# Seven block products in place of eight for three quarters of a decoder trunk's second feed-forward product

## The chip, the core and the metric

The kernel runs on one core of one Trainium2 chip. The metric is the device time of one execution in microseconds (us), as the median over several runs. Engines are written as in the profile: PE is TensorE (matmuls), PEld its loading of the stationary operand, DVE is VectorE, ACT is ScalarE, POOL is GpSimd, and SP is the engine that issues the transfers (SPq in the rows).

## The reference

One layer of a decoder for 512 tokens and a model width of 1024. Four mixers run beside each other, are merged by gates and projected; then comes a feed-forward block. Only its second product is changed.

```python
D_MODEL = 1024; SEQ = 512; D_FF = 4 * D_MODEL
...
x = x + merged @ w_out[l]
h2 = rms_norm(x, norm2_g[l])
x = x + jnp.square(jax.nn.relu(h2 @ w_ff1[l])) @ w_ff2[l]
```

## The kernel before

All products are made with float32 values split in two parts, a rounded high part (`hi`, on ScalarE, L84) and the rest (`lo`, on VectorE, L85). One product of two 128-row tiles is then three matmuls: high by high, high by low, low by high (`mm3`, L143 to L145). Every matmul here streams 512 columns.

Weights come in units. A unit is 512 KB: SP loads it into a tile `raw`, and `load_w` splits that into `whi` and `wlo` (128x1024 each). The list `plan` holds the units in the order of use, and `wunit()` hands out the next one after it has asked for the split of the unit `AHEAD` = 2 places on and for the transfer of one 3 places further. The pool `wp` has three buffers each of `raw`, `whi` and `wlo`, so a split has to wait until TensorE is done with the unit three places back.

The feed-forward block is the last third of the program. Its input `xT` (the normalized tokens, transposed and split) is left by the output projection `w_out`, whose stationary operand is the merged activations `mh`, `ml` and whose moving operand is the weights.

The **first product** (L1156 to L1161) makes 32 tiles of 128 hidden channels by 512 tokens. Tile m is one unit: 24 matmuls into one PSUM bank (`gbank`, a ring of four). Then ScalarE takes relu out of the bank and VectorE multiplies it by the bank's positive part, which gives `y`. The row statistics of the second normalization are not applied here; since relu squared scales with the square of its input, they are applied at the end as one factor `rstd` per token.

The **second product** (L1162 to L1182) has two column halves of 512. In each, four PSUM banks collect 128 tokens each over all 32 channel tiles: 16 weight units, each with two tiles of `y`, which are split into `yy` on the way (64 splits in all, since both halves do it). Per unit 24 matmuls, per half 384. At the end of each half VectorE adds bank times `rstd` to the residual `x2` and SP stores it.

Instructions are put on their engines by a scheduler in about the order in which the code is written; on each engine they then run in that order, and each waits at the head of its queue for what it needs.

Of the kernel before, what the change touches and what calls it, by code (L numbers as in the profile page):

```python
# [11 lines left out]
F32 = mybir.dt.float32  # L12
# [4 lines left out]
ALU = mybir.AluOpType  # L17
# [21 lines left out]
def trunk(ctx, tc, x, positions, norm1_g, w_in, dn_conv_w, dn_a_log, dn_dt_bias, dn_out_norm_g,  # L39
# [22 lines left out]
    wp = ctx.enter_context(tc.tile_pool(name="wp", bufs=3))  # L62
    up = ctx.enter_context(tc.tile_pool(name="up", bufs=1))
    psg = ctx.enter_context(tc.tile_pool(name="psg", bufs=4, space=PSUM))
# [3 lines left out]
    def W(name, tag="tr", dt=F32):  # L68
        return up.tile([P, S], dt, tag=tag, name=name, bufs=BUFS[tag])

# [22 lines left out]
    def spec_b(w2d, c0, nb=1):  # L93
        return [([(0, w2d[:, c0:c0 + nb * P].rearrange("(k p) c -> p k c", p=P))], 8 // nb, nb * P)]
# [11 lines left out]
    def load_raw(i):  # L106
        while len(raws) <= min(i, len(plan) - 1):
            srcs, n, width = plan[len(raws)]
# [4 lines left out]
            raws.append(raw)  # L113

    def load_w(i):
        while len(wts) <= min(i, len(plan) - 1):
            j = len(wts)
            load_raw(j)
            used = plan[j][1] * plan[j][2]
            hi = wp.tile([P, 1024], F32R, tag="whi", name="whi")  # L120
            lo = wp.tile([P, 1024], F32R, tag="wlo", name="wlo")
            split(hi[:, :used], lo[:, :used], raws[j][:, :used])
            wts.append((hi, lo))
# [18 lines left out]
    def mm3(ps, lh, ll, rh, rl, start, stop):  # L142
        T.matmul(out=ps, lhsT=lh, rhs=rh, start=start, stop=False)  # L143
        T.matmul(out=ps, lhsT=lh, rhs=rl, start=False, stop=False)  # L144
        T.matmul(out=ps, lhsT=ll, rhs=rh, start=False, stop=stop)  # L145

# [34 lines left out]
    def mm4(lhsT, rhs):  # L181
        pb = mbank()
        for t in range(NT):
            T.matmul(out=pb[:, tsl(t)], lhsT=lhsT[:, tsl(t)], rhs=rhs[:, tsl(t)], start=True, stop=True)  # L184
        return pb

    def pad(pool, name):
# [75 lines left out]
    rstd1 = small([NT], "rstd1")  # L263
    hb = [[up.tile([P, 4, S], F32R, tag="h", name="h", bufs=4) for _ in range(2)] for _ in range(2)]
    hT = [tuple(hb[k // 4][i][:, k % 4, :] for i in range(2)) for k in range(KC)]
# [84 lines left out]
    for c in range(2):  # L350
        plan += spec_a(w_out[0], [(c * 512, 512)])
    for m in range(32):
        plan += spec_b(w_ff1[0], m * P)
# [784 lines left out]
    ss2 = small([NT, 2], "ss2")  # L1138
    xb = [[up.tile([P, 4, S], F32R, tag="h", name="xT", bufs=4) for _ in range(2)] for _ in range(2)]
    xT = [tuple(xb[k // 4][i][:, k % 4, :] for i in range(2)) for k in range(KC)]  # L1140
    for c in range(2):
# [9 lines left out]
    r2 = small([NT], "rstd2")  # L1151
    V.tensor_tensor(out=r2, in0=ss2[:, :, 0], in1=ss2[:, :, 1], op=ALU.add)
    V.tensor_scalar(out=r2, in0=r2, scalar1=1.0 / D, scalar2=EPS, op0=ALU.mult, op1=ALU.add)
    V.reciprocal(out=r2, in_=r2)
    ys = []
    for m in range(32):  # L1156
        ps, = gemm_b(xT)
        y = W("y", "AQSSGVRU"[m // 4])
        A.activation(out=y, in_=ps, func=AF.Relu)
        V.scalar_tensor_tensor(out=y, in0=ps, scalar=0.0, in1=y, op0=ALU.max, op1=ALU.mult)  # L1160
        ys.append(y)  # L1161
    for c in range(2):  # L1162
        cs_ = slice(c * 512, (c + 1) * 512)
        banks = [gbank() for _ in range(NT)]
        for u in range(16):
            hi, lo = wunit()
            yy = []
            for kk in range(2):
                yh, yl = (pg.tile([P, S], F32R, tag="mg", name="yy", bufs=8) for _ in range(2))
                split(yh, yl, ys[u * 2 + kk])  # L1170
                yy.append((yh, yl))
            order = [(kk, t) for kk in range(2) for t in range(NT)]
            if u == 15:
                order.sort(key=lambda e: (e[1], e[0]))
            for kk, t in order:
                k = u * 2 + kk
                mm3(banks[t], yy[kk][0][:, tsl(t)], yy[kk][1][:, tsl(t)], hi[:, kk * 512:(kk + 1) * 512],
                    lo[:, kk * 512:(kk + 1) * 512], k == 0, k == 31)
# [4 lines left out]
    pg.release()  # L1183

# [29 lines left out]
```

## Time and profile before

| | |
|---|---|
| median of 3 runs | 1053.35 us (1052.5 to 1054.16) |
| the profiled execution | 1054.67 us, of which the span is 1052.9 us |
| granted TensorE clock, mean | 0.995 of full speed |
| first feed-forward product | 698.8 to 873.0 us of the span |
| second feed-forward product | 873.0 to 1049.0 us |

The span runs from the first to the last instruction. An instruction's duration in the profile is not what it adds to the span where it overlaps the next one: matmuls of 0.39 us start every 0.23 us here.

### The profile page before, as it was taken

Reading aid. Unit: us, or ns where it says so; the run is one execution under the profiler, and the core shown is the slowest. Engines: PE = TensorE matmul, PEld = TensorE weight load, DVE = VectorE, ACT = ScalarE, POOL = GpSimd, SP = SyncE. Lnnn points to the kernel's source line nnn. Section 1 sums busy time; section 2 is a strip of 40 time slices with the busy share of each in tenths; the row PEclk is TensorE's granted clock in tenths of the full one; section 3 lists DMA queues with packets and bytes.
Section 4 is the critical chain, followed back from the end, with each engine's and each line's share of the span. In section 5 each row is a group of like instructions: output and inputs, shape, how many; then the busy total and the mean of one; then the engine's idle time right before and its main releaser. Section 6 shows DMA issues by size and latency. Waiting matters only on the chain.

```text
span 1052.9 us, 13056 instructions
## 1 busy us (share of the span) xinstructions
PE 1028.0 (98%) x5067; PEld 848.2 (81%) x5067; DVE 533.3 (51%) x894; ACT 401.6 (38%) x700; POOL 173.0 (16%) x209
## 2 busy tenths in 40 slices
PE   6989989999999989999999999999999999999998
PEld 6868877888888867778888888888888888888886
DVE  6783899623654854432555433444333334445443
ACT  6563334232443542443444233343222223444331
POOL 2553234100300610105342112000000000000000
PEclk9999989999999999999999999999999999999999
DMA  6334333222233221223422433233333333224321
GB/s 195 102 101 110 101 72 90 81 60 63 69 87 113 80 81 48 75 68 91 121 80 60 120 100 100 81 100 99 90 93 99 100 101 94 88 99 140 101 81 40
DMA packets 130886, 96.71 MB, mean 92 GB/s; under 512 B 15924, under 2 KB 112256, under 8 KB 130824
## 3 DMA queue, kind: packets, MB, share of 16 engines
q1 hardware_dynamic: 130744, 95.85, 31.5%
q8 instruction: 40, 0.66, 0.3%
q14 instruction: 22, 0.18, 0.1%
q10 hardware_dynamic: 80, 0.03, 0.0%
HBM read 92.96 MB, written 2.90 MB: 91 GB/s over the span
## 4 chain that ended last, share of the span: by engine, by line
PE 86%; DVE 8%; DMA 2%; issue 2%; POOL 2%; ACT 1%; SPq 0%; POOLq 0%; DVEq 0%; ACTq 0%
PE g L143 25%; PE g L144 25%; PE g L145 25%; PE m L884 2%; PE m L175 1%; DVE wlo L85 1%; PE m L184 1%; PE m L1030 1%; DVE cv L521 1%; PE m L874 1%; DMA raw<-in_w_in_dram 1%; PE m L1029 1%; PE m L1098 1%; DVE D L631 1%; DVE xw L630 1%
## 5 line engine op out<-in xcount | busy, mean ns | idle before, releaser
L85 DVE TENSOR_TENSOR wlo<-raw,whi 128x1024 fp32r<-128x1024 f32 (+2 forms) x160 | 204.9, 1281 | 307.1 <-ACT whi L84 297.7
L84 ACT ACTIVATE whi<-raw 128x1024 fp32r<-128x1024 f32 (+2 forms) x160 | 167.7, 1048 | 368.3 <-PE g L144 234.5
L143 PE MATMUL g<-h,whi 128*128 128x512 f32 x416 | 168.0, 404 | 0.0
L145 PE MATMUL g<-h,wlo 128*128 128x512 f32 x416 | 164.1, 394 | 0.0
L144 PE MATMUL g<-h,whi 128*128 128x512 f32 x416 | 163.3, 393 | 0.0
L144 PE MATMUL g<-wlo,yy 128*128 128x512 f32 x256 | 100.9, 394 | 0.0
L143 PE MATMUL g<-whi,yy 128*128 128x512 f32 x256 | 100.3, 392 | 0.0
L143 PE MATMUL g<-xT,whi 128*128 128x512 f32 x256 | 99.7, 389 | 0.0
L144 PE MATMUL g<-xT,whi 128*128 128x512 f32 x256 | 99.6, 389 | 0.0
L145 PE MATMUL g<-xT,wlo 128*128 128x512 f32 x256 | 99.6, 389 | 0.0
L145 PE MATMUL g<-whi,yy 128*128 128x512 f32 x256 | 99.3, 388 | 0.0
L145 PEld LDWEIGHTS g<-h,wlo 128*128 128x128 f32 x416 | 78.9, 190 | 16.6
L143 PEld LDWEIGHTS g<-h,whi 128*128 128x128 f32 x416 | 79.0, 190 | 16.2 <-issue 0.5
L144 PEld LDWEIGHTS g<-h,whi 128*128 128x128 f32 x416 | 78.9, 190 | 16.1 <-issue 0.5
L85 DVE TENSOR_TENSOR yy<-y,yy 128x512 fp32r<-128x512 f32 x64 | 44.3, 693 | 79.0 <-ACT yy L84 78.6
L84 ACT ACTIVATE yy<-y 128x512 fp32r<-128x512 f32 x64 | 40.4, 632 | 104.1 <-PE g L144 98.4
L837 POOL TENSOR_TENSOR mg<-mg,tg 128x512 f32<-128x512 f32 x24 | 35.7, 1490 | 194.2 <-DVE tg L833 193.8
L143 PEld LDWEIGHTS g<-whi,yy 128*128 128x128 f32 x256 | 48.1, 188 | 11.4 <-DVE y L1160 0.2
L145 PEld LDWEIGHTS g<-whi,yy 128*128 128x128 f32 x256 | 48.1, 188 | 10.8
L145 PEld LDWEIGHTS g<-xT,wlo 128*128 128x128 f32 x256 | 48.1, 188 | 10.1
L144 PEld LDWEIGHTS g<-xT,whi 128*128 128x128 f32 x256 | 48.1, 188 | 10.0
L143 PEld LDWEIGHTS g<-xT,whi 128*128 128x128 f32 x256 | 48.1, 188 | 9.8
(364 smaller groups left out, 1672.6 us busy)
## 6 DMA issues: line engine op xcount, KB each, us to landing
raw<-in_w_in_dram SPq DMA_DIRECT2D x68, 512.0 KB
raw<-in_w_ff_dram SPq DMA_DIRECT2D x64, 512.0 KB
raw<-in_w_branch_dram SPq DMA_DIRECT2D x16, 512.0 KB
raw<-in_w_out_dram SPq DMA_DIRECT2D x8, 512.0 KB
x<-in_x_dram SPq DMA_DIRECT2D x4, 512.0 KB
x<-in_x_dram SPq DMA_DIRECT2D x8, 256.0 KB
out_dram<-x SPq DMA_DIRECT2D x8, 256.0 KB
raw<-in_w_in_dram SPq DMA_DIRECT2D x4, 456.0 KB
```

What stands on the lines that cost most here:

```text
L84: A.activation(out=hi, in_=src, func=AF.Copy)
L85: V.tensor_tensor(out=lo, in0=src, in1=hi.bitcast(F32), op=ALU.subtract)
L143: T.matmul(out=ps, lhsT=lh, rhs=rh, start=start, stop=False)
L144: T.matmul(out=ps, lhsT=lh, rhs=rl, start=False, stop=False)
L145: T.matmul(out=ps, lhsT=ll, rhs=rh, start=False, stop=stop)
L175: T.transpose(out=pb[:, tsl(t)], in_=srcs[t], identity=ident)
L184: T.matmul(out=pb[:, tsl(t)], lhsT=lhsT[:, tsl(t)], rhs=rhs[:, tsl(t)], start=True, stop=True)
L521: V.scalar_tensor_tensor(out=y[:, 3 - k:], in0=ps[:, :n], scalar=par(R_CONV + 12 * k + blkno), in1=y[:, 3 - k:], op0=ALU.mult, op1=ALU.add)
L630: V.tensor_tensor(out=xr, in0=last(UB[:, r, r:], nm), in1=XB[:, r:, m0:], op=ALU.mult)
L631: V.tensor_reduce(out=XB[:, r, m0:], in_=xr.rearrange("p c m -> p m c"), axis=AX.X, op=ALU.add, negate=True)
L837: G.tensor_tensor(out=merged[m], in0=merged[m], in1=tgs[b], op=ALU.add)
L884: T.matmul(out=pv[:, tsl(m)], lhsT=vblk(h, j), rhs=pts[n][:, o_ + j * P:o_ + (j + 1) * P], start=(j == 0), stop=(j == i))
```

## The change

Three quarters of the second product (hidden channels 0 to 3071) are made in three groups of 1024 channels. In a group the product is a 2 by 2 block product: tokens in halves of 256, channels in even and odd tiles of 128, columns in halves of 512. The eight block products are replaced by seven, in Winograd's form of Strassen's scheme: sums and differences of blocks of `y` and of blocks of the weights are made on VectorE, seven products are formed, and sums of those give the result. A block product is two units (halves f of the channels), each of 12 matmuls; so a group has 14 units with 168 matmuls where there were 192. The fourth quarter is computed as before, with its `y` split once and not twice.

The units of group i stand in the plan amid the first product's tiles m = 8i+8 and on (`seq`): 3 units, a tile, 3 units, a tile, 4 units, a tile, 4 units, five tiles. The weights of a group come as four blocks of 1 MB (`re`, `ro`). The weight sums are L232 in the changed program, the sums of `y` L239 to L241 and L247, the additions of the products into `u` or `x2` L277, the last ones L282. The residual is scaled beforehand (ScalarE, L1267) and afterwards (L1296), so that products can be added to it unscaled.

The splits get a fourth pair of buffers (`hilo`) and are asked for three units ahead, not two, from here on.

```diff
+PRODS = (1, 7, 6, 2, 5, 4, 3)
+UNITS = [(1, 0), (7, 0), (1, 1), (7, 1)] + [(p, f) for p in PRODS[2:] for f in range(2)]
...
+dst, a, b, op = {7: (T_, b22, b12, ALU.subtract), 6: (T_, T_, b11, ALU.add),
+                 5: (b12, b12, b11, ALU.subtract), 4: (T_, b21, T_, ALU.subtract)}[p]
+V.tensor_tensor(out=dst, in0=a, in1=b, op=op)
...
+def a_sums(g, f):
+    V.tensor_tensor(out=s1, in0=a21, in1=a22, op=ALU.add)
+    V.tensor_tensor(out=a21, in0=a11, in1=a21, op=ALU.subtract)
+    V.tensor_tensor(out=s2, in0=s1, in1=a11, op=ALU.subtract)
...
+def wunit_mm(g, p, f, dst):
+    hi, lo, ah, al = wunit()
...
+    for q in range(2):
+        for t in range(2):
+            mm3(X[t], ah[:, q, tsl(t)], al[:, q, tsl(t)], hi[:, q * 512:(q + 1) * 512],
+                lo[:, q * 512:(q + 1) * 512], not more and f + q == 0, f + q == 2, more)
...
+        V.tensor_tensor(out=d, in0=d, in1=X[t], op=ALU.add)
...
-        load_w(i + AHEAD)
+        load_w(i + AHEAD + len(whl))
...
+seq = list(range(8))
+for i in range(3):
+    us, m = [(i,) + v for v in UNITS], 8 * i + 8
+    seq += us[0:3] + [m] + us[3:6] + [m + 1] + us[6:10] + [m + 2] + us[10:14] + list(range(m + 3, m + 8))
...
-        for u in range(16):
+        for u in range(12, 16):
             plan += spec_a(w_ff2[0, u * 256:(u + 1) * 256], [(c * 512, 512)], 2)
```

TensorE has 4149 rows where it had 4221, 72 fewer. Ahead of the first tile of the first product all engines have the same instructions with the same waits as before.

The first place is VectorE's queue. Before, in the second product, it holds splits alone, two of `yy` to one of weights:

```order
L85 TENSOR_TENSOR yy_7072<-y_6094,yy_7071 128x512
L85 TENSOR_TENSOR yy_7076<-y_6128,yy_7075 128x512
L85 TENSOR_TENSOR wlo_7028<-raw_6917,whi_7027 128x1024
L85 TENSOR_TENSOR yy_7110<-y_6162,yy_7109 128x512
L85 TENSOR_TENSOR yy_7114<-y_6196,yy_7113 128x512
```

Now, in the second group, between the units that stand around tiles m = 16 and m = 17 (`al` and `wlo` are low parts of a block of `y` and of weights, `T` and `re` weight sums, `S` a sum of `y`, `u` a sum of products, `m` and `g` PSUM banks; the last row is the split for m = 17):

```order
L232 TENSOR_TENSOR T_6778<-T_6778,re_6469 128x1024
L86 TENSOR_TENSOR wlo_6820<-T_6664,whi_6819 128x1024
L86 TENSOR_TENSOR al_6825<-S_6626,ah_6824 128x512
L277 TENSOR_TENSOR u_6240<-u_6240,m_6782 128x512
L277 TENSOR_TENSOR u_6242<-u_6242,m_6783 128x512
L86 TENSOR_TENSOR wlo_6846<-T_6778,whi_6845 128x1024
L86 TENSOR_TENSOR al_6850<-S_6772,ah_6849 128x512
L86 TENSOR_TENSOR al_6903<-y_6244,ah_6902 128x512
L232 TENSOR_TENSOR T_6664<-ro_6590,T_6664 128x1024
L232 TENSOR_TENSOR T_6778<-ro_6592,T_6778 128x1024
L1285 SCALAR_TENSOR_TENSOR y_6844<-g_6853,y_6844 128x512
L86 TENSOR_TENSOR wlo_6881<-raw_6828,whi_6880 128x1024
```

Sums of weights and of products now stand between the splits, and the split of a first-product tile stands behind them.

The second place is SP's queue at the start of the feed-forward block. Before, one transfer of 512 KB follows another (`128x8x128` for the first product, `128x2x512` for the second):

```order
L112 DMA raw<-in_w_out_dram 128x2x512 x8
L112 DMA raw<-in_w_ff_dram 128x8x128 x32
L112 DMA raw<-in_w_ff_dram 128x2x512 x21
L1182 DMA out_dram<-x_5506 128x512
L1182 DMA out_dram<-x_5510 128x512
```

Now the 1 MB blocks of a group stand among the first product's transfers:

```order
L116 DMA raw<-in_w_out_dram 128x2x512 x8
L116 DMA raw<-in_w_ff_dram 128x8x128 x5
L219 DMA re<-in_w_ff_dram 128x2x1024 x2
L219 DMA ro<-in_w_ff_dram 128x2x1024 x2
L116 DMA raw<-in_w_ff_dram 128x8x128 x8
L219 DMA re<-in_w_ff_dram 128x2x1024 x2
L116 DMA raw<-in_w_ff_dram 128x8x128
L219 DMA ro<-in_w_ff_dram 128x2x1024 x2
L116 DMA raw<-in_w_ff_dram 128x8x128 x7
```

The four blocks of the first group are issued ahead of the transfers for tiles m = 5 and on, and each later pair ahead of the transfers that follow it.

## Rows read from the trace of the kernel before

**Rows 1.** The page's head: span, busy time and its share by engine.

```profile
span 1052.9 us, 13056 instructions
PE 1028.0 (98%) x5067; PEld 848.2 (81%) x5067; DVE 533.3 (51%) x894; ACT 401.6 (38%) x700; POOL 173.0 (16%) x209
```

**Rows 2.** Stretches of the two feed-forward products: length, busy times (instructions), clock, DMA.

```profile
core 0: us, PE busy (x) PEld busy (x) DVE busy (x) ACT busy (x) POOL busy (x), PEclk, DMA share, GB/s
699.00:873.00 174.00, 174.00 (x770) 144.06 (x769) 62.88 (x74) 52.68 (x71) 0.00 (x0) 1.00 0.33 97
873.00:1049.00 176.00, 176.00 (x769) 143.96 (x767) 83.75 (x98) 67.04 (x91) 0.00 (x0) 1.00 0.28 90
```

**Rows 3.** Waits from 699 us on: engine, for whom, us in total, times, longest.

```profile
DVE wlo L85 <- ACT whi L84: 117.1, 61, 3.6
ACT whi L84 <- PE g L144: 104.7, 29, 3.9
...
PEld g L143 <- DVE y L1160: 0.2, 1, 0.2
```

**Rows 4.** Timeline of TensorE: start us, us, engine, line (w_out, first product, second product).

```profile
694.02 0.39 PE L145 MATMUL g<-whi,ml 128*128 128x512 f32 x1
...
696.74 0.39 PE L145 MATMUL g<-whi,ml 128*128 128x512 f32 x1
...
698.76 0.49 PE L143 MATMUL g<-xT,whi 128*128 128x512 f32 x1
...
872.99 0.39 PE L143 MATMUL g<-whi,yy 128*128 128x512 f32 x1
...
1048.64 0.39 PE L145 MATMUL g<-whi,yy 128*128 128x512 f32 x1
```

**Rows 5.** Groups by line and form, VectorE and ScalarE, 699 us on: busy, mean ns | idle before.

```profile
L85 DVE TENSOR_TENSOR wlo<-raw,whi 128x1024 fp32r<-128x1024 f32 x62 | 76.0, 1226 | 117.1 <-ACT whi L84 117.1
L85 DVE TENSOR_TENSOR yy<-y,yy 128x512 fp32r<-128x512 f32 x64 | 44.3, 693 | 79.0 <-ACT yy L84 78.6 <-PE g L144 0.4
L1160 DVE SCALAR_TENSOR_TENSOR y<-g,y 128x512 f32<-128x512 f32 x32 | 21.9, 683 | 0.0
...
L84 ACT ACTIVATE whi<-raw 128x1024 fp32r<-128x1024 f32 x61 | 64.3, 1054 | 115.7 <-PE g L144 104.7 <-issue 11.0
L84 ACT ACTIVATE yy<-y 128x512 fp32r<-128x512 f32 x64 | 40.4, 632 | 104.1 <-PE g L144 98.4 <-DVE y L1160 5.6
L1159 ACT ACTIVATE y<-g 128x512 f32<-128x512 f32 x32 | 18.5, 578 | 0.0
```

**Rows 6.** Groups of VectorE before 699 us: an addition out of PSUM, and one beside GpSimd.

```profile
L1144 DVE TENSOR_TENSOR x<-x,g 128x512 f32<-128x512 f32 x8 | 5.3, 684 | 2.5 <-PE g L145 2.5
L649 DVE TENSOR_TENSOR D<-comp,dmask 128x512 f32<-128x512 f32 x4 | 5.1, 1291 | 0.0
```

**Rows 7.** Two stretches at the kernel's start, columns as in rows 2.

```profile
2.00:4.00 2.00, 0.24 (x1) 0.18 (x1) 0.30 (x1) 1.04 (x1) 0.57 (x7) 1.00 0.82 284
4.00:6.00 2.00, 0.00 (x0) 0.00 (x0) 1.01 (x4) 0.72 (x2) 0.23 (x1) 1.00 1.04 369
```

**Rows 8.** Timeline of ScalarE at the start of the first product: its last square of `x2`.

```profile
698.18 0.61 ACT L1150 ACTIVATE sq<-x 128x512 f32<-128x512 f32 x1
```

**Rows 9.** Timeline of TensorE around a wait at 133 us.

```profile
136.29 1.87 PE L538 MATMUL m<-one,sq 128*128 128x1 f32 x8 [3.40 <-ACT sq L535]
...
140.30 0.63 PE L143 MATMUL g<-h,whi 128*128 128x512 f32 x1
...
142.43 0.50 PE L145 MATMUL g<-h,wlo 128*128 128x512 f32 x1
142.78 0.40 PE L143 MATMUL g<-h,whi 128*128 128x512 f32 x1
143.01 0.40 PE L144 MATMUL g<-h,whi 128*128 128x512 f32 x1
```

**Rows 10.** The stretch around that wait, columns as in rows 2.

```profile
131.00:158.00 27.00, 23.60 (x122) 20.32 (x121) 24.76 (x37) 8.76 (x13) 9.87 (x7) 0.87 0.36 71
```

More of the change, by code (lines that the diff above doesn't have):

```diff
@@ L113, in load_raw, with load_t, hilo @@
             raws.append(raw)
+    srcs_w, whl = [], []
+    def load_t(i):
+        while len(srcs_w) <= min(i, len(plan) - 1):
+            e = plan[len(srcs_w)]
+            srcs_w.append(w_src(*e) if isinstance(e[0], dict) else None)
+    def hilo(j):
+        if whl and j % 4 == 3:
+            return (whl[0].tile([P, 1024], F32R, tag="w" + n, name="w" + n, bufs=1) for n in ("hi", "lo"))
+        return (wp.tile([P, 1024], F32R, tag="w" + n, name="w" + n) for n in ("hi", "lo"))
     def load_w(i):
@@ L185, in mm4, with wgroup, wload @@
         return pb
+    PRODS = (1, 7, 6, 2, 5, 4, 3)
+    UNITS = [(1, 0), (7, 0), (1, 1), (7, 1)] + [(p, f) for p in PRODS[2:] for f in range(2)]
+    XOF = {1: 1, 2: 1, 6: 2, 7: 3, 4: 3, 5: 4, 3: 4}
+    fps = []
+    def wgroup(w2d):
+        return dict(w=w2d, e=[], o=[], T={}, S1={}, S2={}, y=[], X={})
+    def wload(g, e):
+        for f in range(2):
+            t = fps[0].tile([P, 2, 1024], F32, tag="r" + "eo"[e], name="r" + "eo"[e], bufs=2)
+            SY.dma_start(out=t, in_=g["w"][f * 512:(f + 1) * 512].rearrange("(q e p) c -> e p q c", e=2, p=P)[e])
+            g["eo"[e]].append(t)
@@ new lines, in trunk @@
+    US = []
+    def wunit_mm(g, p, f, dst):
+        hi, lo, ah, al = wunit()
+        x = XOF[p]
+        more = p in (2, 4, 3)
+        if not more and f == 0:
+            g["X"][x] = [gbank() if x in (2, 4) else mbank() for _ in range(2)]
+        X = g["X"][x]
+        for q in range(2):
+            for t in range(2):
+                mm3(X[t], ah[:, q, tsl(t)], al[:, q, tsl(t)], hi[:, q * 512:(q + 1) * 512],
+                    lo[:, q * 512:(q + 1) * 512], not more and f + q == 0, f + q == 2, more)
+        if f == 0:
+            return
+        for t in range(2):
+            if p in (1, 7) and len(US) < 4:
+                US.append(fps[0].tile([P, 512], F32, tag="u", name="u", bufs=4))
+                A.activation(out=US[-1], in_=X[t], func=AF.Copy)
+                continue
+            d = US[t] if p in (1, 6) else US[2 + t] if p == 7 else dst(
+                *{2: (t, 0), 5: (2 + t, 1), 4: (2 + t, 0), 3: (t, 1)}[p])
+            V.tensor_tensor(out=d, in0=d, in1=X[t], op=ALU.add)
@@ L187, in pad, with wfold @@
+    def wfold(dst):
+        for t in range(2):
+            for d, v in ((dst(t, 1), US[t]), (dst(2 + t, 0), US[t]), (US[2 + t], US[t]), (dst(2 + t, 1), US[2 + t])):
+                V.tensor_tensor(out=d, in0=d, in1=v, op=ALU.add)
     def pad(pool, name):
@@ L263, in trunk @@
     rstd1 = small([NT], "rstd1")
[L264 removed]
+    hb = [[hp.tile([P, 4, S], F32R, tag="h", name="h", bufs=4) for _ in range(2)] for _ in range(2)]
     hT = [tuple(hb[k // 4][i][:, k % 4, :] for i in range(2)) for k in range(KC)]
@@ L1150, in trunk, with dst @@
             A.activation(out=s_, in_=x2[t][c], func=AF.Square, accum_out=ss2[:, t, c:c + 1])
[L1151 to L1161, printed above, removed]
+    mr = small([2, NT], "rstd2")
+    ms2, r2 = mr[:, 0, :], mr[:, 1, :]
+    V.tensor_tensor(out=ms2, in0=ss2[:, :, 0], in1=ss2[:, :, 1], op=ALU.add)
+    V.tensor_scalar(out=ms2, in0=ms2, scalar1=1.0 / D, scalar2=EPS, op0=ALU.mult, op1=ALU.add)
+    V.reciprocal(out=r2, in_=ms2)
+    up.release()
+    pg.release()
+    fps.append(ctx.enter_context(tc.tile_pool(name="fp", bufs=1, reuse_waits="tile")))
+    py = tc.alloc_tile_pool(name="py", bufs=3, side="right", reuse_waits="tile")
+    whl.append(fps[0])
+    for e in range(2):
+        wload(gF[0], e)
+    for c in range(2):
+        for t in range(NT):
+            A.activation(out=x2[t][c], in_=x2[t][c], func=AF.Copy, scale=ms2[:, t:t + 1])
+    def dst(t, c):
+        return x2[t][c]
+    ys = [[], [], [], []]
+    for g, y_ in zip(gF, ys):
+        g["y"] = y_
+    for e in seq:
+        if isinstance(e, int):
+            f, q = e // 4 % 2, e % 4
+            if q == 0:
+                ys[e // 8].append(py.tile([P, 2, 2, S], F32, tag="y", name="y", bufs=3))
+                if e == 0:
+                    pad(py, "pady")
+            ps, = gemm_b(xT)
+            y = ys[e // 8][f][:, q // 2, q % 2, :]
+            A.activation(out=y, in_=ps, func=AF.Relu)
+            V.scalar_tensor_tensor(out=y, in0=ps, scalar=0.0, in1=y, op0=ALU.max, op1=ALU.mult)
+            if q == 3 and e < 24:
+                a_sums(gF[e // 8], f)
+        else:
+            i, p, f = e
+            wunit_mm(gF[i], p, f, dst)
+            if i < 2 and f == 1 and p in (5, 3):
+                wload(gF[i + 1], int(p == 3))
+    wfold(dst)
+    for c in range(2):
+        for t in range(NT):
+            A.activation(out=x2[t][c], in_=x2[t][c], func=AF.Copy, scale=r2[:, t:t + 1])
+    yy = []
     for c in range(2):
```

75 lines of the change are left out of this document (54 added, 21 removed).

## The prediction

> **What bounds the kernel now.** I read the page first: TensorE is busy for 98% of the span, VectorE for 51%, ScalarE for 38% [rows 1]. Shares over a whole span hide stages, so I cut out the two feed-forward products [rows 2]. In both TensorE is busy without a break at a granted clock of 1.00 (its upper level, 2.4 GHz). VectorE works 36% of the first product (62.88 of 174) and 48% of the second, ScalarE 30% and 38%, GpSimd not at all. The list of waits says the same from the other side: VectorE waits 117 us for ScalarE's `whi`, ScalarE 105 us for TensorE to give a buffer free, while TensorE's only wait in 350 us is one of 0.2 us [rows 3]. So here the time is the number of matmuls times the step from one start to the next, and everything else has room.
>
> The step is not the 0.39 us in a row, since neighbours overlap; it comes from starts [rows 4]. First product: 768 matmuls from 698.76 to 872.99, 0.2269 us each. Second: 767 steps from 872.99 to 1048.64, 0.2290 each. The output projection, whose operands have the same parts as those of a block product (activations loaded, weights streamed): 12 steps in 2.72 us, 0.2267. No row says why the second product's step is 1% longer.
>
> **What goes.** Three groups have 504 matmuls in place of 576; the last quarter keeps its 192. Before: 768 x 0.2290 = 175.9 us. After: for the block products I take the projection's step, 504 x 0.2267 = 114.3 us, and for the last quarter the middle of both steps, 43.8 us. That is 158.1 us, so **17.8 us** go. The bounds: 0.2267 for all 696 gives 18.1; 0.2290 for all gives 16.5; and if the longer step is caught by the first product's tiles too, which now stand between block products, another 1.6 us is lost, 14.9. I take 17.7, near the upper end, because the projection is the nearest row.
>
> The Trainium skill (TensorE: Matmul & The Clock Gate, Back-to-back issue gap) gives about 131 ns for each pair of weight load and matmul of 512 columns in a sustained stream. By it 72 matmuls would be worth only 9.4 us; the steps here are 227 to 229 ns, and the measurement decides.
>
> **What is added.** Per group, on VectorE, with durations of [rows 5, 6]: 22 `wlo` (14 units, 8 tiles) at 1.226, 14 `al` of 512 elements like `yy` at 0.693, 8 weight sums, 8 sums of `y`, 8 `y` at 0.683, 14 additions out of PSUM at 0.684. The sums in this form are not in the trace. A weight sum has two float32 operands in SBUF and 1024 elements, as `wlo` has, so I take 1.226, and 0.693 for a sum of `y`. Below that nothing in the rows goes. Above is the 1.291 us that a product of 512 took while GpSimd worked [rows 6], about double; GpSimd is idle here [rows 2], so I stay at the lower end. The sum is 27.0 + 9.7 + 9.8 + 5.5 + 5.5 + 9.6 = 67 us per group, against 8 tiles at 5.44 and 168 matmuls, 81.6 us, on TensorE: 82%. ScalarE: 22 x 1.054 + 14 x 0.632 + 8 x 0.578 = 36.6 us, 45%. So on average there is cover. Without that cover 67 us per group would come on top, 201 in all.
>
> The average is not enough, because a group's 14 units stand close together: a unit is 2.72 us on TensorE, and its preparation and additions take VectorE 3.7 us on average. The cover is the lead of three units. I walked the queue through the tightest place of the printed order, with zero at the end of tile 15 of the first product. TensorE: three units, tile 16, three units, 8.2 + 5.4 + 8.2, so tile 17 starts at 21.8. VectorE can begin `wlo` of tile 16 when its buffer is free and ScalarE has made `whi`, at 1.1. Behind it stand, up to `wlo` of tile 17: `y`, 3 sums of `y`, 3 `wlo`, 4 `al`, 3 weight sums, 2 additions, `y`, and that `wlo` itself. With the first it is 8 x 1.23 + 7 x 0.69 + 4 x 0.68 = 17.4 us, done at 18.5. What each waits for (`whi`, a free buffer, the end of a product) comes earlier by the same walk. So the split is **3.3 us early**; the following one (unit 1 of product 2) is needed at 27.2 and done at 21.1; tile 18 is early by about 5 us. In the third group the 8 last additions, 8 splits of `yy` and ScalarE's scalings come in as well, but the order puts them into the 3 to 5 us that the later units leave, and none at the border to the last quarter. VectorE would have to be 19% slower than these rows before TensorE waits.
>
> **Transfers.** Bytes are the same. What moves is when: four blocks of 1.05 MB go out at the block's start, the first two when the projection has ended (about 697), the others after ScalarE's last square at 698.8 [rows 8]. At the start of the kernel the queues moved 284 and 369 GB/s [rows 7]; the 97 GB/s of the first product is what was asked for. At 330, 4.2 MB take 13 us, so the last lands near 712. Behind it wait two weight sums in VectorE's queue, and behind these `y` of tile 1 and the split of tile 5: four sums and that split, 6.2 us, done by about 719, and tile 5 starts at 698.8 + 5 x 5.44 = 726. Seven microseconds to spare. SP's transfers for tiles 5 and on stand behind the blocks and land by 715. In later groups an `re` pair goes when product 5 is split, an `ro` block when product 3 is; I count 5 us between its landing and the tile behind it.
>
> **The sum.** 1054.67 - 17.7 = 1037.0 us for the profiled execution (a span of 1035.2); that one stood 1.3 above the median, so the median becomes 1053.35 - 17.7 = **1035.7 us**. The end (four additions, stores) is unchanged.
>
> **Rivals.**
> *VectorE is late here and there.* For: 3.3 us is not much, and one late split holds TensorE at once. Against: rows of one form agree to a few ns, and the walk uses them. If the sums take a third more than rows say, or starts lag 0.2 us behind each release, the place above loses 3 to 4 us per group and TensorE waits up to 1 to 4 us there: 3 to 12 us in all, 1039 to 1048.
> The price of a wait can double. A wait of 3.40 us near 133 us was followed by matmuls 0.43 us apart, 140.30 to 142.43, in place of 0.23 [rows 9]; the granted clock over that stretch was 0.87 [rows 10]. So some time at 1.2 GHz follows such a wait, here five steps of 0.2, 1 us. The Trainium skill (TensorE: Matmul & The Clock Gate, What's actually happening) has the lower rate as the state of an idle array; the trace agrees.
> *VectorE becomes the bound: slower.* Its queue runs in order, and an addition at its head waits for TensorE to end a product while the next units' splits stand behind. If that uses up the lead, a unit costs VectorE's 3.7 us and not 2.72: 14 x 1.0 = 14 us per group, 42 in all, less 17.7: 1078. It decides from 5.9 us of TensorE waits per group. Against: in the walk no addition is reached before its product is done.
> *The blocks come late.* If 97 GB/s were what this stage can get, 4.2 MB would take 43 us; VectorE would stand before the first sums until 740, tile 5 would start at about 745 and not 726, and 17.7 us would be gone: 1054, no change. Against: the rates of [rows 7].
> That the change does not do what it says can't be: TensorE has 72 matmuls fewer.
>
> **Chances.** Forecast (no wait to speak of) 0.66, own range 1034.9 to 1038.5. VectorE late here and there 0.20, 1039 to 1048. Bound by VectorE 0.06. Blocks late 0.05. Another loss 0.03. The time, 1035.7, is the forecast's. The range of 8 in 10 takes the forecast and two thirds of the first rival: 1034.7 to 1044. A change below 0.2% (2.1 us) can't be told from none in this kernel. Faster: 0.66 + 0.20 + 0.01 = 0.87; within 0.2%: 0.04, mostly the late blocks; slower: 0.09.
>
> **What the profile will show.** If right: TensorE has no idle time from 699 us to the end, the last matmul starts near 1031; block products step by 0.2267 to 0.2290; weight sums take 1.23 us and sums of `y` 0.69; VectorE is busy 72% there (about 240 of 332 us). If wrong: TensorE waits for `wlo` or `al`, first at tiles 9, 17 and 25; or VectorE's `T` waits for a transfer beyond 716; or sums beyond 1.5 us; or a granted clock below 1.00 in this stage.

## The result and the profile after

| | before | after |
|---|---|---|
| median | 1052.92 us (4 runs, 1051.31 to 1054.16) | 1034.47 us (4 runs, 1033.37 to 1035.78) |
| ratio | | 0.9826 (95% interval 0.9808 to 0.9844) |
| profiled execution | 1054.67 us, span 1052.9 | 1034.64 us, span 1032.9 |

The change takes 18.4 us off (16.4 to 20.2 by the interval), where 17.7 were forecast. The time lies 0.2 us under the low end of the range, 1034.7. The four times before are the three behind the earlier median of 1053.35 and one more, 1051.31. The page's head answers to [rows 1]: TensorE has 4995 matmuls where it had 5067, 72 fewer, and keeps its 98%; VectorE has gone from 51% to 59%.

```profile
span 1032.9 us, 12908 instructions
PE 1010.1 (98%) x4995; PEld 833.9 (81%) x4995; DVE 610.0 (59%) x992; ACT 422.8 (41%) x724; POOL 172.8 (17%) x210
```

The stretches of the feed-forward block, with the columns of [rows 2], show where: VectorE is busy for 223 of 332 us, and the clock stays at 1.00.

```profile
699.00:873.00 174.00, 174.00 (x769) 144.12 (x768) 127.75 (x154) 80.92 (x107) 0.00 (x0) 1.00 0.36 117
873.00:1031.00 158.00, 156.29 (x689) 128.90 (x687) 94.70 (x115) 58.43 (x75) 0.00 (x0) 1.00 0.23 72
```

The stretch 873:1031 reaches beyond the last matmul, so its 1.7 us of idle TensorE are the end, not a wait. The list of waits of that block, which answers to [rows 3], says so directly. TensorE has one wait, of 0.3 us, 3 us into the last quarter, for a bank that the last `y` sets free:

```profile
DVE wlo L86 <- ACT whi L85: 78.1, 39, 4.2
ACT whi L85 <- PE g L165: 48.3, 21, 4.1
...
PEld g L164 <- DVE y L1285: 0.3, 1, 0.3
```

The timeline of TensorE answers to [rows 4]: the first matmul of the first product, the first block product and a matmul ten steps later, the first matmul of tile 17, the first of the last quarter, and the last of all.

```profile
697.00 0.48 PE L164 MATMUL g<-xT,whi 128*128 128x512 f32 x1
...
740.63 0.39 PE L164 MATMUL m<-whi,ah 128*128 128x512 f32 x1
...
742.90 0.39 PE L165 MATMUL m<-wlo,ah 128*128 128x512 f32 x1
...
843.99 0.39 PE L164 MATMUL g<-xT,whi 128*128 128x512 f32 x1
...
985.43 0.39 PE L164 MATMUL g<-whi,yy 128*128 128x512 f32 x1
...
1028.90 0.39 PE L166 MATMUL g<-whi,yy 128*128 128x512 f32 x1
```

The block of matmuls is 1028.90 - 697.00 = 331.90 us long, against 1048.64 - 698.76 = 349.88 before: **17.98 us less**. The other 2.0 us between the two profiled spans lie outside it: 1.76 in front, where the programs have the same instructions, and 0.26 behind the last matmul. The steps of the second product are now 0.2267 us: ten from 740.63 to 742.90 in a block product, and the same in the last quarter but for its wait (191 steps from 985.43 to 1028.90, 43.47 us).

VectorE's groups (697 us to the end) give the durations that [rows 5, 6] had stood for:

```profile
L86 DVE TENSOR_TENSOR wlo<-raw,whi 128x1024 fp32r<-128x1024 f32 x38 | 46.5, 1223 | 40.4 <-ACT whi L85 40.3
...
L277 DVE TENSOR_TENSOR x<-x,m 128x512 f32<-128x512 f32 x12 | 7.7, 681 | 0.0
...
L232 DVE TENSOR_TENSOR T<-ro,re 128x1024 f32<-128x1024 f32 x6 | 7.3, 1219 | 0.0
...
L239 DVE TENSOR_TENSOR S<-y 128x512 f32<-128x512 f32 x6 | 4.2, 693 | 0.2
```

### The profile page after: what moved, and what is told of

It reads as the page before. It is cut to its first block, busy times and chain, and to the rows that moved or that the text cites. A ratio compares the mean times of both kernels' runs of the same rounds, so it can differ in the third digit from the quotient of the medians.

```text
span 1032.9 us, 12908 instructions
## 1 busy us (share of the span) xinstructions
PE 1010.1 (98%) x4995; PEld 833.9 (81%) x4995; DVE 610.0 (59%) x992; ACT 422.8 (41%) x724; POOL 172.8 (17%) x210
## 4 chain that ended last, share of the span: by engine, by line
PE 86%; DVE 8%; DMA 2%; issue 1%; ACT 1%; POOL 1%; SPq 0%; ACTq 0%; DVEq 0%; POOLq 0%
PE g L164 23%; PE g L166 23%; PE g L165 23%; PE m L164 2%; PE m L165 2%; PE m L166 2%; PE m L986 2%; DMA raw<-in_w_in_dram 2%; PE m L196 1%; DVE wlo L86 1%; PE m L205 1%; PE m L1132 1%; DVE cv L623 1%; PE m L976 1%; PE m L1131 1%
## 5 line engine op out<-in xcount | busy, mean ns | idle before, releaser
L86 DVE TENSOR_TENSOR wlo<-raw,whi 128x1024 fp32r<-128x1024 f32 (+2 forms) x136 | 175.4, 1290 | 229.0 <-ACT whi L85 219.6
L85 ACT ACTIVATE whi<-raw 128x1024 fp32r<-128x1024 f32 (+2 forms) x136 | 142.7, 1049 | 319.3 <-PE g L165 155.3
L164 PE MATMUL g<-whi,h 128*128 128x512 f32 x128 | 50.8, 397 | 0.0
L166 PE MATMUL g<-whi,h 128*128 128x512 f32 x128 | 49.9, 390 | 0.0
L165 PE MATMUL g<-wlo,h 128*128 128x512 f32 x128 | 49.9, 389 | 0.0
L164 PE MATMUL m<-whi,ah 128*128 128x512 f32 x96 | 37.3, 389 | 0.0
L165 PE MATMUL m<-wlo,ah 128*128 128x512 f32 x96 | 37.3, 389 | 0.0
L166 PE MATMUL m<-whi,al 128*128 128x512 f32 x96 | 37.3, 389 | 0.0
L86 DVE TENSOR_TENSOR wlo<-T,whi 128x1024 fp32r<-128x1024 f32 x18 | 22.0, 1220 | 11.5 <-ACT whi L85 11.4
```

The costliest lines, as they stand in the source:

```text
L85: A.activation(out=hi, in_=src, func=AF.Copy)
L86: V.tensor_tensor(out=lo, in0=src, in1=hi.bitcast(F32), op=ALU.subtract)
L164: T.matmul(out=ps, lhsT=lh, rhs=rh, start=start, stop=False, skip_group_check=more)
L165: T.matmul(out=ps, lhsT=lh, rhs=rl, start=False, stop=False, skip_group_check=more)
L166: T.matmul(out=ps, lhsT=ll, rhs=rh, start=False, stop=stop, skip_group_check=more)
```

## Experiments

Each kernel was timed against the kernel before, and one execution was profiled. "The block" is the time from the first feed-forward matmul to the last; before it is 349.88 us, after 331.90. A step is the mean over all starts of its kind.

### Where the 18 us come from

**Eight products again, in the new order.** In `wunit_mm` the matmuls of product 1 are issued twice:

```diff
+        for r in range(2 if p == 1 else 1):
+            for q in range(2):
...
-                    lo[:, q * 512:(q + 1) * 512], not more and f + q == 0, f + q == 2, more)
+                        lo[:, q * 512:(q + 1) * 512], not more and f + q + r == 0,
+                        f + q == 2 and r == (p == 1), more or p == 1)
```

> The changed kernel with the matmuls of the first block product of each group issued twice into the same banks, so that a group has 192 matmuls again (that product then enters the result doubled); everything else as in the changed kernel. Theory (the gain is the matmuls): 72 x 0.2267 = 16.3 us longer than the changed kernel, about 1050.8, which is the kernel before less 1.7 us of step. Rival (a part of the gain came from the fewer splits of y or from the earlier transfers): clearly less than 16 us longer, 1048 or under.

Measured: 1051.26 us, ratio 0.9984 (0.9974 to 0.9993); the block 348.24. The 72 matmuls are worth 16.34 us in the block, 0.2269 each, and nothing else of the new order costs or brings anything. The Trainium skill (TensorE: Matmul & The Clock Gate, Back-to-back issue gap) has about 131 ns for a pair of weight load and matmul of this size, from which an estimate for 72 is 9.4 us; this run, with 16.34, does not bear that out. What is left to the kernel before is 1.64 us of the block; the next run shows that it is the share of the shorter step.

**The step of the second product.** The kernel before, with `yy` in buffers that lie lower in SBUF:

```diff
-                yh, yl = (pg.tile([P, S], F32R, tag="mg", name="yy", bufs=8) for _ in range(2))
+                yh, yl = WR("yy", ("cv", "tr")[kk])
```

> The kernel before, with one thing changed: the split activations of the second product (yy) lie in buffers lower in SBUF that are free by then, in place of those at its upper end. Theory (the longer step of 0.2290 us came from where the loaded operand lies): the second product steps by 0.2267 us, its 768 matmuls take 174.1 us and not 175.9, and the time falls by 1.7 us, ratio 0.9984. Rival (it came from the form of the loop, from the values, or from the work of the other engines): the step stays at 0.2290 and the time within 0.5 us of before.

Measured: 1051.57 us, ratio 0.9986 (0.9978 to 0.9995); the block 348.17, 1.71 less, and the 768 matmuls step 0.2268 apart. The block is then that of the run with eight products to 0.1 us. So the longer step in [rows 4] came from where `yy` lay. Why that place was slow, this run can't say: it changes the height in SBUF and the start address's divisors at once.

### What sets the step

**The pools exchanged.** The changed kernel with the new buffers at the upper end of SBUF, and `y` where they were:

```diff
-    fps.append(ctx.enter_context(tc.tile_pool(name="fp", bufs=1, reuse_waits="tile")))
-    py = tc.alloc_tile_pool(name="py", bufs=3, side="right", reuse_waits="tile")
+    fps.append(tc.alloc_tile_pool(name="fp", bufs=1, side="right", reuse_waits="tile"))
+    py = tc.alloc_tile_pool(name="py", bufs=3, reuse_waits="tile")
...
```

> The changed kernel with the same instructions in the same order, but with the new tiles laid out from the other end of SBUF, so that the split blocks of y (ah, al) lie at its upper end, as yy did before; yy of the last quarter stays lower. Theory of the place: the 504 matmuls of the block products step by 0.2290 us in place of 0.2267, the last quarter and the first product stay at 0.2267; 1.2 us longer than the changed kernel, about 1035.7. Rival (not the place): all steps 0.2267 and 1034.5.

Measured: 1039.35 us, ratio 0.9874 (0.9859 to 0.9889); the block 337.69, 5.8 more than after. That is a miss for the theory that the upper end is slow by 1%: the block products step 0.2325 apart on average, the tiles of the first product whose `whi` and `wlo` are the fourth pair step 0.233 too, while their neighbours stay at 0.2267, and `yy` of the last quarter, which lies low, steps 0.2323, where my expectation had 0.2267. That pair does not lie at the upper end: it starts at byte 176096, beside the 175872 where `ah` is fast in the changed kernel. What the slow operands share in the compiled program is a start address that is no multiple of 256 bytes. Hence the next five runs.

**`yy` at the upper end, on a multiple of 256.** The kernel before, with 192 bytes more ahead of `yy`:

```diff
-    def pad(pool, name):
-        G.memset(pool.tile([P, 8], F32, name=name, bufs=1), 0.0)
+    def pad(pool, name, n=8):
+        G.memset(pool.tile([P, n], F32, name=name, bufs=1), 0.0)
...
-    pad(pg, "padg")
+    pad(pg, "padg", 56)
```

> The kernel before with 192 bytes more ahead of its buffers yy, so that these start at byte 204544 of a partition (799 x 256) and not at 204736, still at the upper end. If the start address of an operand, by the power of two that divides it, sets TensorE's step (the alignment theory): the 768 matmuls of the second feed-forward product step .2267 us apart and not .2290, 1.7 us less in all, a ratio of .9984. If the place at the upper end sets it (the place theory): steps of .2290 and no change of time, a ratio of 1.000.

Measured: 1051.69 us, ratio 0.9991 (0.9981 to 1.0001). By the time alone this is not told from no change, but the block is: 348.18 us with steps of 0.2268, the same as with `yy` lower down. The height in SBUF plays no part here.

**Block products off that multiple, by 64, 32, 192 and 128 bytes.** The changed kernel, with a pad ahead of `ah`, `al` and `u` (n = 16, 8, 48 or 32 floats), ahead of the first split of a block:

```diff
+        if not g["X"] and p == 1 and f == 0 and g is gF[0]:
+            pad(fps[0], "pads", n)
...
```

> The changed kernel with 64 bytes more ahead of the buffers of S and T (ah, al) and of u, so that the 504 matmuls of the block products read operands that start at odd multiples of 64 bytes. Alignment theory: those matmuls step .2290 us apart, 1.2 us more in all, 1035.6 us. Place theory: .2267, no change, 1034.5 us. Either way no engine is waited for.

> The changed kernel with 32 bytes more at the same place, so that the operands of the block products start at odd multiples of 32 bytes. Alignment theory: the 504 matmuls step .2333 us apart, or .2283 for some, as they did in the run with the pools exchanged, 2 to 3.3 us more in all, 1036.5 to 1037.8 us. Place theory: .2267, no change, 1034.5 us.

> The changed kernel with 192 bytes more ahead of ah and al, the offset against multiples of 256 bytes that yy had in the kernel before. If the offset alone sets the step: .2290 as there, 1.2 us more, 1035.7 us. If every offset but 0 costs the block products .2333, as 32 and 64 bytes did: 3.3 us more, 1037.8 us, and what made .2290 of it in the kernel before stays open.

> The changed kernel with 128 bytes more at the same place. If only multiples of 256 bytes are read at the fast step: .2290 to .2333 for the 504 matmuls, 1035.7 to 1037.8 us. If multiples of 128 are enough: .2267, 1034.5 us.

Measured, with start addresses as the compiled programs have them:

| kernel | stationary operand, first byte | beyond a multiple of 256 | its step, us | block, us | time, us (interval of the ratio) |
|---|---|---|---|---|---|
| before | `yy` 204736 | 192 | .2290 | 349.88 | 1052.92 |
| before, `yy` moved | `yy` 204544 | 0 | .2268 | 348.18 | 1051.69 (0.9981 to 1.0001) |
| after | `ah` 175872 | 0 | .2267 | 331.90 | 1034.47 (0.9808 to 0.9844) |
| off by 32 | `ah` 175904 | 32 | .2332 | 335.35 | 1038.83 (0.9859 to 0.9893) |
| off by 64 | `ah` 175936 | 64 | .2333 | 335.59 | 1037.75 (0.9846 to 0.9880) |
| off by 128 | `ah` 176000 | 128 | .2324 | 334.91 | 1038.02 (0.9845 to 0.9875) |
| off by 192 | `ah` 176064 | 192 | .2290 | 333.05 | 1035.60 (0.9828 to 0.9855) |
| pools exchanged | `ah` 204768 | 224 | .2325 | 337.69 | 1039.35 (0.9859 to 0.9889) |

In all rows but the last the moving operand starts on a multiple of 256. There the start of the stationary one sets the step, in `yy` and `ah` alike: 192 gives 0.2290 in both. My expectation that each halving of the power of two makes it worse was wrong: 64 costs 0.2333, not 0.2290, and 128 costs nearly as much as 32.

The stationary operand is not alone in this, as the kernel with the pools exchanged shows. Some of its units have the fourth pair as the moving operand, and then both operands start 224 bytes beyond a multiple. There the step goes back to 0.2267. In its last quarter the unit that ends at 1000.02 is such a one, ten steps in 2.27 us; in the next one the weights start on a multiple again, and ten steps take 2.34:

```profile
997.75 0.39 PE L165 MATMUL g<-wlo,yy 128*128 128x512 f32 x1
...
1000.02 0.39 PE L166 MATMUL g<-whi,yy 128*128 128x512 f32 x1
1000.24 0.40 PE L164 MATMUL g<-whi,yy 128*128 128x512 f32 x1
...
1002.58 0.39 PE L165 MATMUL g<-wlo,yy 128*128 128x512 f32 x1
```

In its block products the same holds: 0.2333 with the weights on a multiple, and 0.2267 behind the first five steps of a unit whose weights start at 224, which together makes the 0.2325 of the table. So what these kernels share is a fast step where both operands start equally far beyond a multiple of 256, and a longer one where they do not. Only the distances 0 and 224 were seen in both operands, and no run has a moving operand off the multiple with a stationary one on it.

In the timeline of the kernel off by 64, ten steps of the first block product take 2.33 us, where in the changed kernel they take 2.27:

```profile
740.72 0.40 PE L164 MATMUL m<-whi,ah 128*128 128x512 f32 x1
...
743.05 0.40 PE L165 MATMUL m<-wlo,ah 128*128 128x512 f32 x1
```

No duration shows it. The loading of the stationary operand has 188 ns in that kernel (groups of PEld, 740 to 1000 us; the columns end with busy time, mean ns and idle time before),

```profile
L165 PEld LDWEIGHTS m<-wlo,ah 128*128 128x128 f32 x95 | 17.9, 188 | 4.3
```

and the same in the changed kernel, where only the idle time in front is shorter:

```profile
L165 PEld LDWEIGHTS m<-wlo,ah 128*128 128x128 f32 x96 | 18.0, 188 | 3.7
```

### How much room VectorE had

**Each weight sum two, three and four times.** The extra sums go to a buffer that nobody reads; n is 1, 2 or 3:

```diff
+        for _ in range(n):
+            z = fps[0].tile([P, 2, 512], F32, tag="z", name="z", bufs=1)
+            V.tensor_tensor(out=z, in0=a, in1=b, op=op)
         V.tensor_tensor(out=dst, in0=a, in1=b, op=op)
```

> The changed kernel with each weight sum made twice on VectorE (the first into a tile that nobody reads): 24 more instructions of 1.1 to 1.2 us, three of them in the tightest place. Theory: 3.4 us of the 4.6 us to spare go, no wait of TensorE to speak of: 1034 to 1036. Rival (no room on VectorE): up to 28 us more, 1040 or above.

> The changed kernel with each weight sum made three times on VectorE: 48 more instructions, six of them in the tightest place, 6.8 us against 4.6 us to spare. Theory: TensorE now waits, first at tiles 9, 17 and 25, 2 to 4 us per group, and if a wait is long enough some matmuls follow at the lower clock: 1040 to 1047. Rival (VectorE has much more room than the walk says): still 1034 to 1036.

> Each of the 24 weight sums made four times, three of them into a buffer that nobody reads. From the run with three: 48 sums more had made VectorE 53.4 us busier (1.11 each) without a wait of TensorE, and left it busy for 193.2 of the 205 us from 699 to 904. The third set more adds 22.9 us there: 216.2 us of work in 205 us, 11 us too much. If VectorE bounds the products once its work passes TensorE's 82 us per group, TensorE waits 4 to 10 us in all (what VectorE was ahead by comes off the 11): 1039 to 1045 us. If something else hid the sums of the run with three: no waits, 1035 us.

Measured: 1034.74 (0.9812 to 0.9847), 1034.96 (0.9814 to 0.9852) and 1049.87 us (0.9957 to 0.9986). With three sums my expectation failed: TensorE had no wait but the 0.3 us that the changed kernel has too, and the block stayed at 331.91. One reason is that the extra sums did not go where I had put them. I had six between the splits for tiles 16 and 17; the timeline of VectorE has one there (`z`), and two weight sums beside it where the changed kernel has three:

```profile
825.16 1.23 DVE L86 TENSOR_TENSOR wlo<-raw,whi 128x1024 fp32r<-128x1024 f32 x1
...
837.99 1.22 DVE L234 TENSOR_TENSOR z<-ro,T 128x1024 f32<-128x1024 f32 x1
...
839.86 1.22 DVE L86 TENSOR_TENSOR wlo<-raw,whi 128x1024 fp32r<-128x1024 f32 x1
```

The second split ends at 841.08 and tile 17 starts at 845.81, 4.7 us later, as in the changed kernel. The scheduler has moved the rest to places with room. So this run loads VectorE as a whole and not its tightest place. The stretches show how full it is (columns as in [rows 2]): VectorE works 77 to 80 of 82 us beside the block products, and TensorE is busy throughout.

```profile
740.00:822.00 82.00, 82.00 (x363) 67.90 (x362) 77.26 (x86) 37.09 (x49) 0.00 (x0) 1.00 0.33 103
822.00:904.00 82.00, 82.00 (x363) 67.92 (x362) 79.71 (x91) 34.64 (x44) 0.00 (x0) 1.00 0.33 103
904.00:985.00 81.00, 81.00 (x359) 67.05 (x359) 69.40 (x86) 41.94 (x56) 0.00 (x0) 1.00 0.22 65
```

With four it is over the edge. VectorE is idle for 1 to 2 us of each stretch, and TensorE makes 34 and 32 matmuls fewer in the later two; it is idle for 4 and 5.5 us of them, and in part of the first its clock is lower:

```profile
699.00:740.00 41.00, 41.00 (x182) 33.97 (x181) 36.21 (x40) 18.20 (x27) 0.00 (x0) 1.00 0.41 132
740.00:822.00 82.00, 82.00 (x362) 67.70 (x362) 81.04 (x90) 36.71 (x49) 0.00 (x0) 1.00 0.33 103
822.00:904.00 82.00, 78.06 (x329) 61.66 (x328) 80.10 (x91) 31.99 (x41) 0.00 (x0) 0.98 0.33 103
904.00:985.00 81.00, 75.50 (x327) 60.43 (x326) 80.19 (x93) 39.13 (x51) 0.00 (x0) 1.00 0.17 52
```

Its waits are on `wlo` and `al`, as the prediction had it for a late VectorE, and most of all on ScalarE's `whi`, which in turn waits for VectorE's sums `T` (14.3 us) and, three times, for a transfer of weights (9.3 us), which in the changed kernel it never does:

```profile
ACT whi L85 <- DVE T L235: 14.3, 4, 6.1
...
ACT whi L85 <- DMA raw<-in_w_ff_dram: 9.3, 3, 3.7
...
PEld g L164 <- ACT whi L85: 5.6, 6, 1.6
...
PEld m L164 <- ACT whi L85: 2.9, 2, 2.3
PEld m L166 <- DVE al L86: 2.9, 2, 1.4
PEld m L165 <- DVE wlo L86: 2.7, 4, 1.0
```

The block is 347.73 us, 15.8 longer, where I had 4 to 10. Up to 904 that holds: TensorE has made 35 matmuls fewer than with three sums, 8 us. Another 32, 7.3 us, are lost in 904:985, which my sum had left out. VectorE comes into that stretch with work left over (197 of the 216 us are done by 904) and is busy for 80 of its 81 us.

**Without the fourth pair of buffers**, so that splits lead by two units and not three:

```diff
     py = tc.alloc_tile_pool(name="py", bufs=3, side="right", reuse_waits="tile")
-    whl.append(fps[0])
```

> The changed kernel without the fourth pair of buffers and with a lead of two units, as the kernel before had. Theory (VectorE's queue has room; after the change the split for tile 17 ended 4.6 us before its tile began): one unit less of lead takes 2.7 us away, 1.9 us stay; no wait of TensorE to speak of, 1034 to 1036. Rival (the lead is what keeps TensorE busy): TensorE waits for wlo at tiles 9, 17 and 25 and between the units, 2 to 5 us per group, 1041 to 1050.

Measured: 1035.44 us, ratio 0.9836 (0.9814 to 0.9858); the block 331.91, no wait. The third unit of lead covers nothing here.

**All 14 units of a group in a row**, the first product's tiles behind them:

```diff
-        seq += us[0:3] + [m] + us[3:6] + [m + 1] + us[6:10] + [m + 2] + us[10:14] + list(range(m + 3, m + 8))
+        seq += us + list(range(m, m + 8))
```

> The changed kernel with the 14 units of each group in a row, with no tile of the first product between them; the eight tiles follow. Theory as the prediction had it (a unit costs VectorE 3.7 us): 14 us more than TensorE needs per group, less a lead of 8 us: 6 us per group, 18 in all, about 1052. Rival, from the packed rows after the change (1.14 us for a split, 0.60 for a small one, 3.1 us per unit): 5 us more than TensorE needs, all inside the lead: 1034 to 1037.

Measured: 1034.63 us, ratio 0.9829 (0.9810 to 0.9848); the block 332.26, three waits of 0.1 us. Even so, VectorE keeps up.

### Further in the same direction

**All four quarters by seven products.** The last quarter becomes a fourth group, its units at the end:

```diff
-    gF = [wgroup(w_ff2[0, i * 1024:(i + 1) * 1024]) for i in range(3)]
+    gF = [wgroup(w_ff2[0, i * 1024:(i + 1) * 1024]) for i in range(4)]
...
+    seq += [(3,) + v for v in UNITS]
...
```

> The changed kernel with the last quarter in seven block products too, its 14 units standing in a row behind the last tile of the first product, and the final scaling and stores behind them. Theory (matmuls decide while VectorE is covered): 24 matmuls fewer, 5.4 us; at the end the last additions, the folds, the scalings and all eight stores stand bare, about 4 us, and VectorE's packed 3.1 us per unit against 2.72 us on TensorE costs 0 to 4 us: 1031 to 1037, about 1034. Rival (VectorE bounds units that stand in a row): 14 us for the 14 units and 4 us at the end less 5.4: 1045 or more.

Measured: **1030.81 us**, ratio 0.9791 (0.9776 to 0.9806), the fastest kernel of this study. The block is 326.44 us, 5.46 less than after, 24 matmuls at 0.2275. Behind the last matmul 6.9 us are left, not 4.0 as after. VectorE's and ScalarE's last rows stand in a line there, between the last matmul (1022.38) and the end (1029.3):

```profile
1022.12 1.37 DVE L277 TENSOR_TENSOR x<-x,g 128x512 f32<-128x512 f32 x2 [0.20 <-PE g L166]
1023.41 1.89 DVE L282 TENSOR_TENSOR x<-x,u 128x512 f32<-128x512 f32 x3
...
1024.13 1.95 ACT L1294 ACTIVATE x<-x,rstd 128x512 f32<-128x512 f32 x3 [2.03 <-DVE x L282]
```

**The same with a shorter end**: folds after product 6, six tiles scaled and stored after product 4, and the last product added straight into the other two:

```diff
+            if p == 3 and g is gF[3]:
+                V.scalar_tensor_tensor(out=dst(t, 1), in0=X[t], scalar=r2[:, t:t + 1], in1=dst(t, 1),
+                                       op0=ALU.mult, op1=ALU.add)
+                SY.dma_start(out=out[0, tsl(t), 512:1024], in_=dst(t, 1))
+                continue
...
+            if i == 3 and (p, f) == (6, 1):
+                wfold(dst)
...
```

> All four quarters by seven block products, with another end: six of the eight output tiles are added up, scaled and stored while the last products run, and the last product is scaled and added straight into the two tiles that are left. TensorE has 672 matmuls as in the run with four quarters, 326.4 us. If the 6.9 us behind the last matmul of that run were the folds, scalings and stores that stood in a row there, 4 us or so remain, as in the changed kernel: about 1028 us, 2 to 3 us under 1030.8. If they are the store's own latency: 1030 to 1031 us. If the folds now put in the middle hold up VectorE's sums or TensorE's banks, waits of TensorE of a microsecond and more show in the last 30 us and the time rises.

Measured: 1032.78 us, ratio 0.9815 (0.9801 to 0.9829). The end did shrink, to 1032.3 - 1028.02 = 4.3 us. But the block grew to 329.58: the folds now stand in VectorE's queue ahead of the last sums and splits, it is busy 23.68 us from 1004 to 1030, and TensorE gets waits. The stretch, and two of its waits:

```profile
1004.00:1030.00 26.00, 23.59 (x94) 16.34 (x92) 23.68 (x33) 12.58 (x17) 0.00 (x0) 1.00 0.19 71
```

```profile
PEld g L164 <- ACT ah L85: 1.4, 2, 0.7
PEld g L166 <- DVE al L86: 1.0, 3, 0.4
```

What is saved at the end (2.6 us) is lost a few microseconds earlier (3.1). Block and end together are 333.9 us against 333.3, so the traces show that the shorter end brings nothing. That it costs 2 us, as the medians have it, is not shown: the profiled execution reached the block 2.5 us later (698.44 against 695.94), which is not of its making, and the two intervals overlap. Of the two I would keep the one with four groups and the plain end.

## Why the prediction was right or wrong

**What bounds the kernel: right.** Time is matmuls times step. With 72 matmuls put back, 16.34 of the block's 17.98 us return; the rest is the step of the second product.

**What goes: right, and rounded down.** For the block products I chose 0.2267 and that is what they show (504 x 0.2267 = 114.3). The reason I gave, that the projection loads activations and streams weights too, was not the cause: the second product before did the same at 0.2290. "For the last quarter the middle of both steps, 43.8 us" had the step wrong, since these matmuls go at 0.2267 too; the one wait hides that, and 191 steps take 43.47 us, where the middle gives 43.5. The first product went from 0.2269 to 0.2268. Unrounded, the terms give 17.86 us, and the block lost 17.98; the forecast took 17.7 of it. The missing reason, "no row says why the second product's step is 1% longer", is now known in part: `yy` started 192 bytes beyond a multiple of 256 and the weights on one, and the change happens to put all its operands on such multiples. That the layout came out so is luck, worth 1.6 us. Had the pools been laid out otherwise, up to 5.8 us of the gain would have gone (the pools exchanged), which is more than the 14.9 us bound allowed for.

**The step that failed: the base and the end, not the mechanism.** "So the median becomes 1053.35 - 17.7 = 1035.7" took a median of three runs as if it were exact. With one run more it is 1052.92, and four later series of 9 to 23 runs have 1052.5 to 1052.9. That is 0.43 of the 1.23 us between 1035.7 and 1034.47. The second term is "the end (four additions, stores) is unchanged", which put at nothing what was not worked out: from the start of the last matmul to the end of the span it is 1052.9 - 1048.64 = 4.3 us before and 1032.9 - 1028.90 = 4.0 after, 0.3 less, and the same 4.3 to 4.5 and 4.0 to 4.1 us stand in the other traces with the one end or the other. VectorE's last row starts 0.43 us behind the last matmul in both (1049.07 and 1029.33), so it is the last store that ends sooner; why stays open. The block gave 0.28 more than 17.7. The other 0.2 can't be told from scatter, and the time missed the low end, 1034.7, by no more than that.

The scatter is known better than I made use of. The four runs of either kernel spread by 2.4 to 2.9 us, and over the 17 profiled executions of this study the first feed-forward matmul starts anywhere from 695.69 to 699.10 us, with the same instructions in front. It goes with the granted clock: of 62 later runs of the kernel before, the 20 with a mean clock of 0.997 took 1051.6 us on average, the 29 with 0.995 took 1053.2, the 7 with 0.993 took 1053.8. What makes the clock differ from run to run is not shown. The low end should have had about a microsecond for this; it had 0.55 below the smallest time that the terms gave.

**What is added: covered, with more room than forecast.** Durations were right: weight sums 1.22 us (1.23 forecast), sums of `y` 0.69, additions 0.68. The sum of durations was still too large, because instructions overlap: VectorE was busy 60 to 62 us in the 82 of a group, not 67, and 223 us in all, not 240:

```profile
740.00:822.00 82.00, 82.00 (x363) 67.92 (x362) 59.98 (x70) 36.74 (x48) 0.00 (x0) 1.00 0.33 103
822.00:904.00 82.00, 82.00 (x363) 67.94 (x362) 62.18 (x74) 34.90 (x45) 0.00 (x0) 1.00 0.33 103
```

The timeline of VectorE at the first sums shows it: rows of 1.22 start 1.13 apart, rows of 0.68 are followed after 0.61.

```profile
708.22 1.22 DVE L232 TENSOR_TENSOR T<-ro,re 128x1024 f32<-128x1024 f32 x1
709.35 0.68 DVE L1285 SCALAR_TENSOR_TENSOR y<-g,y 128x512 f32<-128x512 f32 x1
709.96 1.22 DVE L232 TENSOR_TENSOR re<-re 128x1024 f32<-128x1024 f32 x1
711.09 1.22 DVE L232 TENSOR_TENSOR T<-ro,re 128x1024 f32<-128x1024 f32 x1
...
713.48 1.22 DVE L86 TENSOR_TENSOR wlo<-raw,whi 128x1024 fp32r<-128x1024 f32 x1
...
823.35 1.22 DVE L86 TENSOR_TENSOR wlo<-raw,whi 128x1024 fp32r<-128x1024 f32 x1 [2.22 <-ACT whi L85]
...
838.16 1.21 DVE L86 TENSOR_TENSOR wlo<-raw,whi 128x1024 fp32r<-128x1024 f32 x1
```

The prediction had seen the same for TensorE and took starts there; for VectorE it took durations. The last row is the split for tile 17: it ends at 839.37, and the tile starts at 843.99, 4.6 us early where the walk had 3.3. With 1.13 and 0.61 in the walk it would have been about 5. "VectorE would have to be 19% slower" was too low for the same reason: from the row at 823.35 (the split for tile 16) to 839.37 it is 16.0 us, and 4.6 to spare are 29% of that, an estimate that no run tests. What the runs with more sums show is the room on average, with the scheduler free to place them: 24% more work (53.4 us on 222.45) cost nothing, 36% (three more sets at 1.11 us each, 80 us) cost 15.8 us.

**Transfers: early enough, by more than forecast.** The second pair of sums ran at 711.09 behind no transfer, and the split for tile 5 (the row at 713.48) was done at 714.7, not 719. In the ten microseconds behind the projection the queues moved 414 GB/s, not 330:

```profile
696.00:706.00 10.00, 10.00 (x51) 8.31 (x50) 5.32 (x10) 9.79 (x18) 0.00 (x0) 1.00 1.02 414
```

The Trainium skill (Perfetto Trace Analysis, Roofline) lets a single core draw up to about 435 GB/s through its 16 DMA engines; the row stays under that.

**The rivals.** *VectorE late here and there* did not occur; with sums added it comes between 24% and 36% more work, and the run with four sums shows it, with waits on `wlo` and `al` as described and a clock of 0.98 in one stretch. *VectorE the bound* is that same run: real as a mechanism, far from this kernel. *Blocks late* is refuted by the row above.

**What the profile would show.** The last matmul started at 1028.90, not 1031; 1.8 us of that is the earlier start of the block. TensorE had no waits on `wlo` or `al`, `T` none on transfers, and the clock was 1.00, as forecast.

## What to carry to other kernels

Where TensorE never waits, a change of its work is worth matmuls times step, and the step is read from starts; compare the step of the stages first, since a stage with a longer one may only need its stationary operand moved to a multiple of 256 bytes, where the moving one starts too (1.7 us here, for one pad). Sum the work of an engine that must stay hidden by the distance between starts of neighbours as well, and find its room by doubling one kind of its work until something waits; then look in the timeline where the added work was put. Give a range the spread of the base it starts from, and work out the end as well as the middle.

## What the runs showed of the hardware

- The step of a float32 matmul of 512 columns depends on where its two operands start. With the moving operand on a multiple of 256 bytes it is 0.2267 us with the stationary one on a multiple too, 0.2290 at 192 beyond it, and 0.2324 to 0.2333 at 32, 64, 128 and 224. With both 224 beyond, it is 0.2267 again. The loading of the stationary operand has 188 ns in the slow and the fast kernel. Why 192 is cheaper than 128 stays open, and a moving operand off the multiple by itself was not tried.
- VectorE's rows overlap: 1.22 us long, 1.13 apart; 0.68 long, 0.61 apart.
- The queues of this one core moved 414 GB/s over 10 us.
- Ahead of the feed-forward block the same instructions ended between 695.69 and 699.10 us from one execution to another (17 of them); runs of one kernel with a mean granted clock of 0.997 were 1.5 us shorter on average than those with 0.995.
